# A two-layer decoder in split fp32: the first MLP's step list with chunk 0 behind the settling, twelve pairs and eight accumulating transfers

## The chip, the cores and the metric

The kernel runs on one core of one Trainium2 chip. Its engines are PE (TensorE: matrix products), DVE (VectorE), ACT (ScalarE), POOL (GpSimd) and SP (SyncE, which issues the transfers). Each engine takes its own instructions in the order in which they were written for it, and waits on semaphores for the others. SBUF is the on-chip memory, PSUM the eight banks of 128 x 512 fp32 that PE writes its sums to. The metric is device time in microseconds (us); the kernel before takes 544.23 us, the median of three runs (544.15 to 544.59).

## The reference

Two layers, each an attention and an MLP; each of the four parts ends in a residual sum and a LayerNorm. The sequence is 256 tokens of 1024 features, the hidden width of the MLP is 4096. The attentions (block-sparse in layer 0, dilated in layer 1) are not touched by the change in what they do.

```python
def sq_relu_mlp(x, w_in, w_out):
    return jnp.square(jax.nn.relu(x @ w_in)) @ w_out

    ...
    h = x
    for i in range(DEPTH):
        ...
        h = layer_norm(DEEPNORM_ALPHA * h + mix, ln_mix_g[i], ln_mix_b[i])
        h = layer_norm(DEEPNORM_ALPHA * h + sq_relu_mlp(h, mlp_w_in[i], mlp_w_out[i]),
                       ln_mlp_g[i], ln_mlp_b[i])
```

## The kernel before

**Split fp32.** PE gets every fp32 operand as two fp32r parts, a high part (`hi`, a copy in the shorter format) and a low part (`lo`, what is left), and forms three products: hi by hi, hi by lo, lo by hi. So each weight tile costs ACT one copy (`whi<-raw`) and DVE one subtraction (`wlo<-raw,whi`), both 128 x 1024, after SP has loaded it into one of six `raw` buffers. The parts lie in ten `whi` and ten `wlo` slots (`NSLOT`); a new weight waits until PE is done with the one ten earlier. `load_w(..., by_dma=True)` makes the low part in another way: ACT writes -hi into `wlo` (line 414) and a POOL transfer adds the weight to it in memory (line 416), so DVE is not needed; a tile so loaded has the letter `d` in the step list.

**The order of work.** Every operation is recorded with its buffers, and `Plan.order` schedules all of them by written-down costs and latencies: on each engine the operation that can start first comes first, and of several the one with the earliest due time. `NUDGE` shifts the due times of single operations by their number. The result is a fixed order for each engine; the tile names in it carry the number of the buffer.

**The MLP.** Its hidden width is cut into eight chunks of 512, each of four tiles of 128 columns. The step list of `STEPS`, one string for each layer's MLP, is read by `Mlp.rest`:

- Chunk 0's first product runs in `head` and `half`, token by token, half of the 256 tokens at a time.
- `w1` multiplies chunk 1's four tiles by x in four of the PSUM banks called `tp`; `f30` multiplies one tile (chunk 3, tile 0) in one of the four banks called `acc`. For each tile ACT copies half of the bank (`tz<-acc`) and DVE adds the other half (`tz<-acc,tz`), which frees the bank. After every second tile ACT takes relu, the square and the high part (`ahi`), DVE the low part (`alo`).
- `00` is the plain second product of chunk 0's first two tiles of 128 hidden features: 24 matmuls of 128 x 512 into the four sums `acc[m][n]` (token half m, output half n).
- `1A` and `1B` are the second product of chunk 1's first and second two tiles as a Strassen-like pair: seven products of 128 x 512 for eight, so 21 matmuls. They need sums of weights (`load_pair`) and of activations (`side_sums`; their parts lie in `e` buffers) from DVE, and add up in four side banks (the four `tp`) and three of the `acc` sums. The fourth, `acc[1][1]`, is not used by a pair.
- `.3` lets PE do three of the pair's seven products that wait in `todo`, which spreads them between the `f` tiles.
- `drain` adds `acc[1][1]` to the residual and gives its bank free: it is then the one bank through which all `f` tiles rotate. One `f` tile can start only when DVE has added the one before it out of that bank.
- `settle` brings the four side banks into the residual `xtok` (`tok` in the profile).
- Plain steps behind it are not multiplied at their place but collected in `tail`; `out_and_ln` does them output piece by output piece, so that the LayerNorm of the first 128 tokens can begin while PE still works on the others.

## Time and profile before

| | |
|---|---|
| median of three runs | 544.23 us (544.15 to 544.59) |
| profiled execution | 544.48 us |
| span of its trace | 542.7 us |
| granted TensorE clock | 0.997 |
| busy: PE, DVE, ACT, POOL | 534.1, 511.8, 376.8, 12.3 us |
| first MLP's second products and tiles | some 133 to 283 us of the span |
| second MLP's | some 390 to 535 us |

The page of the profile gives busy times, the chain of work that ended last, and groups of instructions by line (a helper's line stands for all that call it, so tiles say more than lines). The timeline lists the instructions of an engine in order of time; like neighbours are merged, with their count at the end. Its first number is the start in us, its second the duration. Matmuls overlap, so the time that one costs is the distance from its start to the next start, not its duration. In brackets stands how long the engine had been idle, and what released it.

### The profile page before, as it was taken

What the parts mean: (1) busy time and instruction counts of PE and PEld (TensorE: products, weight loads), DVE (VectorE), ACT (ScalarE), POOL (GpSimd) and SP (SyncE); (2) the same over time, 40 slices, a digit from 0 to 9 for tenths busy, and PEclk for the clock granted to TensorE, in tenths of its full rate; (3) what the DMA queues carried; (4) which work ended last, traced back from release to release, by engine and by line L of the source; (5) the groups of instructions that cost most, each with busy time, mean ns of one, the idle gap of its engine ahead of it and who ended that gap; (6) DMA issues with size and microseconds to landing.
All of it is one profiled execution on the core that took longest, in us unless ns stands there. A gap on an engine that the chain in (4) does not pass through costs nothing.

```text
span 542.7 us, 9038 instructions
## 1 busy us (share of the span) xinstructions
PE 534.1 (98%) x3398; PEld 452.9 (83%) x3398; DVE 511.8 (94%) x839; ACT 376.8 (69%) x616; POOL 12.3 (2%) x19
## 2 busy tenths in 40 slices
PE   9999999999999999999999999999999999999994
PEld 7888888888888888888878988888888888888883
DVE  6899999798999999999899899989999999999997
ACT  6778786477776797787653655655877879797650
POOL 0000000000000000000000000000000000000001
PEclk9999999999999999999999999999999999999998
DMA  8994245629364678853853841654936685695412
GB/s 319 397 327 171 93 165 187 242 79 338 114 202 169 224 206 270 281 149 122 309 234 105 322 143 57 201 184 152 351 117 194 198 268 167 192 294 208 148 39 77
DMA packets 31259, 108.78 MB, mean 200 GB/s; under 512 B 3440, under 2 KB 4464, under 8 KB 31216
## 3 DMA queue, kind: packets, MB, share of 16 engines
q1 hardware_dynamic: 29952, 104.87, 55.8%
q0 software_dynamic: 864, 3.15, 3.0%
q8 instruction: 26, 0.43, 0.3%
q10 hardware_dynamic: 400, 0.20, 0.1%
q14 instruction: 17, 0.14, 0.1%
HBM read 107.15 MB, written 1.05 MB: 199 GB/s over the span
## 4 chain that ended last, share of the span: by engine, by line
PE 98%; DVE 1%; issue 0%; DVEq 0%
PE acc L390 66%; PE tp L390 29%; PE tp L722 1%; PE tp L739 1%; DVE tok L639 1%; DVE bst L994 0%; DVE bst L978 0%; DVE bst L972 0%; DVEq L1518 0%; DVE tok L632 0%; DVE mv L1008 0%; DVE bst L997 0%
## 5 line engine op out<-in xcount | busy, mean ns | idle before, releaser
L381 ACT ACTIVATE whi<-raw 128x1024 fp32r<-128x1024 f32 (+2 forms) x180 | 181.8, 1035 | 51.8 <-PE acc L390 24.1
L386 DVE TENSOR_TENSOR wlo<-raw,whi 128x1024 fp32r<-128x1024 f32 (+2 forms) x180 | 210.0, 1194 | 5.3 <-ACT whi L381 3.5
L390 PE MATMUL acc<-xs,whi 128*128 128x512 f32 (+1 forms) x560 | 136.1, 387 | 0.0
L390 PEld LDWEIGHTS acc<-xs,whi 128*128 128x128 f32 x560 | 103.6, 190 | 22.2 <-ACT whi L381 0.7
L390 PE MATMUL acc<-xs,wlo 128*128 128x256 f32 x544 | 76.3, 283 | 0.0
L390 PEld LDWEIGHTS acc<-xs,wlo 128*128 128x128 f32 x544 | 73.1, 192 | 3.6
L390 PE MATMUL acc<-whi,ahi 128*128 128x512 f32 (+1 forms) x151 | 55.4, 394 | 0.0
L390 PE MATMUL acc<-wlo,ahi 128*128 128x512 f32 (+1 forms) x151 | 55.1, 388 | 0.0
L390 PE MATMUL acc<-whi,alo 128*128 128x512 f32 (+1 forms) x151 | 54.7, 388 | 0.0
L390 PE MATMUL tp<-whi,e 128*128 128x512 f32 x138 | 48.5, 390 | 0.0
L390 PEld LDWEIGHTS acc<-whi,alo 128*128 128x128 f32 x151 | 28.4, 188 | 6.3 <-DVE alo L632 0.4
L390 PEld LDWEIGHTS acc<-whi,ahi 128*128 128x128 f32 x151 | 28.1, 188 | 6.0 <-ACT ahi L1075 0.4
L390 PEld LDWEIGHTS acc<-wlo,ahi 128*128 128x128 f32 x151 | 28.4, 188 | 5.4
L381 ACT ACTIVATE whi<-m 128x1024 fp32r<-128x1024 f32 x23 | 24.3, 1056 | 12.3 <-DVE m L632 11.2
L632 DVE TENSOR_TENSOR tz<-acc,tz 128x256 f32<-128x256 f32 x68 | 27.9, 418 | 3.3 <-ACT tz L647 2.5
L390 PE MATMUL tp<-xs,whi 128*128 128x512 f32 x128 | 30.2, 391 | 0.0
L390 PEld LDWEIGHTS tp<-whi,e 128*128 128x128 f32 x138 | 26.0, 188 | 5.1
L390 PE MATMUL acc<-whi,xs 128*128 128x512 f32 (+1 forms) x112 | 28.7, 364 | 0.0
L386 DVE TENSOR_TENSOR wlo<-m,whi 128x1024 fp32r<-128x1024 f32 x23 | 28.0, 1218 | 0.1
L390 PEld LDWEIGHTS tp<-xs,whi 128*128 128x128 f32 x128 | 23.9, 188 | 4.9
L632 DVE TENSOR_TENSOR m<-raw,raw 128x1024 f32<-128x1024 f32 x23 | 27.9, 1215 | 0.0
L390 PE MATMUL tp<-wlo,e 128*128 128x512 f32 x69 | 27.0, 392 | 0.0
(127 smaller groups left out, 825.0 us busy)
## 6 DMA issues: line engine op xcount, KB each, us to landing
raw<-in_win_dram SPq DMA_DIRECT2D x64, 512.0 KB, 4.6
raw<-in_wout_dram SPq DMA_DIRECT2D x64, 512.0 KB, 5.0
raw<-in_wqk_dram SPq DMA_DIRECT2D x24, 512.0 KB, 5.6
raw<-in_wo_dram SPq DMA_DIRECT2D x14, 512.0 KB, 3.4
raw<-in_wv_dram SPq DMA_DIRECT2D x8, 512.0 KB, 8.1
wlo<-in_win_dram POOLq DMA_DIRECT2D x6, 512.0 KB, 9.4
g<-in_lng_dram SPq DMA_DIRECT2D x4, 512.0 KB, 6.5
b<-in_lnb_dram SPq DMA_DIRECT2D x4, 512.0 KB, 7.1
```

Of the source, the lines that this page charges most:

```text
L381: op("ACT", act(n, sbuf=sbuf), lambda: nc.scalar.activation(hi(), src(), AF.Copy), r, whi, keen=keen)
L386: lambda: nc.vector.tensor_tensor(lo(), src(), f32(hi()), op=ALU.subtract), list(r) + list(whi), wlo,
L390: nc.tensor.matmul(out_ap, lhsT, rhs, start=start, stop=stop)
L632: op("DVE", dve(n) + extra, lambda: nc.vector.tensor_tensor(out_ap(), a(), b(), op=alu), r, w)
L639: lambda: nc.vector.scalar_tensor_tensor(dst(), a(), s(), b(), op0=o0, op1=o1), r, w,
L722: nc.tensor.transpose(ps.t[:, c : c + P], src(), ident.t)
L739: nc.tensor.transpose(ps.t[:, 32 * i : 32 * i + 32], src()[c, :], ident.t[c, c])
```

## The change

The step list of the first MLP is replaced; that of the second stays.

- `00` and `01` go behind `settle`. Nothing is in the four sums before the pairs, so `drain` goes too, and the banks of the sums are taken only when the first product needs them (`bank(m, n)`). The plain tail becomes chunk 0 and chunk 7, eight k-tiles, where it was six (`61 70 71`); which plain steps are tail is now told by `settled`, not by `TAIL`.
- Chunk 2 is still multiplied as a whole, but as `W2`: into the four `acc` banks, not the `tp` banks, which the pairs now take as soon as chunk 1 has left them.
- All of chunks 1 to 6 are pairs: twelve, where chunk 6's second half was plain.
- Eight `f` tiles are loaded with the accumulating transfer, where two were.
- Chunk 0's activations must now last through the whole MLP. They lie in two of four `e` buffers of 2 x 512, which replace eight of 512; the pairs' activation sums and the attentions' probabilities get halves of such buffers (`Part`). This holds for both MLPs.
- The table `NUDGE` is another one altogether, for numbers from 222 to 2436 in place of 385 to 2447, so that the order shifts in both layers.

```diff
--- before.py
+++ after.py
@@ class Plan: which accesses of a buffer depend on each other
+class Part:
+
+
+    def __init__(self, buf, k):
+        self.buf, self.k = buf, k
+
+    @property
+    def t(self):
+        return self.buf.t[:, self.k, :]
+
+
+def touches(a, b):
+    if a is None or b is None or a == b:
+        return True
+    if isinstance(a, tuple) and isinstance(b, tuple) and a[0] == b[0] == "part":
+        return a[1] == b[1] and (a[2] is None or b[2] is None or a[2] == b[2])
+    return False
+
...
+                if isinstance(b, Part):
+                    b, key = b.buf, ("part", b.k, key)
-                    if key is None or k is None or k == key:
+                    if touches(k, key):
...
 STEPS = (
-    "w1 00 w2 01 drain f30 1A .3 f31 .3 f32 1B .3 f33 .4 f40 2A .3 f41 .3 f42 2B .3 f43 .4 f50 3A .3 f51 .3 f52d "
-    ".3 f53 3B .4 f60 .3 f61 4A .3 f62d .3 f63 4B .4 f70 .3 f71 5A .3 f72 .3 f73 5B .4 6A settle 61 70 71 ",
+    "w1 W2 f30 1A .4 f31d 1B .4 f32 .4 f33d 2A .5 f40 .4 f41d 2B .4 f42 3A .4 f43d .5 f50 3B .4 f51d .4 f52 4A .4 "
+    "f53d 4B .5 f60 .4 f61d 5A .4 f62 .4 f63d 5B .5 f70 6A .4 f71 .4 f72 6B .4 f73 .4 settle 00 01 70 71 ",
     "w1 00 w2 01 drain f30 1A .4 f31 1B .4 f32d .4 f33 2A .5 f40 .4 f41 2B .4 f42d 3A .4 f43 .5 f50 3B .4 f51 .4 "
     "f52d 4A .4 f53 4B .5 f60 .4 f61 5A .4 f62d .4 f63 5B .5 f70 6A .4 f71 .4 f72 6B .4 f73 .4 settle 70 71 ",
 )
...
-    385: 20.75, 418: 9.25, 468: 14.55, 593: 6.3, 604: 12.3, 891: 10.55, 907: 1.65, 974: 12.15, 1032: -14.25, 1046:
...
+    222: 5.95, 237: 6.85, 244: 5.15, 604: 2.8, 717: -5.4, 763: 25.95, 771: -17.45, 788: 19.1, 797: 9.15, 805:
...
-            hi, lo = [mk([P, 512], F32R, "e", 8) for _ in range(2)]
+            t = mk([P, 2, 512], F32R, "e", 4)
+            hi, lo = [Part(t, k) for k in range(2)]
...
-    def mm_pair(act, sums, weights, acc, side, last):
+    def mm_pair(act, sums, weights, bank, side, last):
...
             lambda: product(pure(0, 0), full[0], 0, p1),
-            lambda: product(mixed(1), full[0], 512, acc[0][1][0]),
+            lambda: product(mixed(1), full[0], 512, bank(0, 1)),
             lambda: product(mixed(2), full[1], 0, p5),
             lambda: product(mixed(0), full[1], 512, p7),
             lambda: product(mixed(3), full[2], 0, p6),
-            lambda: product(pure(1, 0), full[2], 512, acc[0][0][0]),
-            lambda: product(pure(1, 1), tail, 0, acc[1][0][0]),
+            lambda: product(pure(1, 0), full[2], 512, bank(0, 0)),
+            lambda: product(pure(1, 1), tail, 0, bank(1, 0)),
         ]
...
-            self.chunks = {c: act_tiles() for c in range(nx)}
+            self.chunks = {c: tuple(mk([P, 4, S], F32R, "e", 4) for _ in range(2)) for c in range(nx)}
...
-            acc = new_acc()
-            side = [psum("tp") for _ in range(4)] if "w" not in STEPS[i] else None
+            acc, side, settled = [[None, None] for _ in range(2)], None, False
+
+            def bank(m, n):
+                if acc[m][n] is None:
+                    acc[m][n] = (psum("acc"), n * 512, 512)
+                return acc[m][n][0]
+
             nkt = DFF // P
-            ntail = TAIL[2 * i + 1]
             tail, sums, todo, boths = [], {}, [], {}
             steps = STEPS[i].split()
             left = len(WPAIRS[i])
@@ -1155,11 +1185,11 @@
 
             plain_left = sum(x[0].isdigit() and x[1] in "01" for x in steps[: steps.index("drain")]) if "drain" in steps else 0
             for step in steps:
-                if step[0] == "w":
+                if step[0] in "wW":
                     c = int(step[1])
                     opened(c)
                     ws = [load_w(win[i][c * 4 + j]) for j in range(4)]
-                    pss = [psum("tp") for _ in range(4)]
+                    pss = [psum("tp" if step[0] == "w" else "acc") for _ in range(4)]
                     mm_wide(pss, ws)
                     for j, ps in enumerate(pss):
                         squared(c, j, ps)
@@ -1174,32 +1204,34 @@
                 elif step[0] == ".":
                     some(int(step[1:]))
                 elif step == "drain":
-                    z, bank = xtok[1], acc[1][1][0]
-                    stt(512, 0, lambda: z.t[:, 512:], lambda: z.t[:, 512:], lambda: ALPHA, lambda: bank.t, ALU.mult, ALU.add,
-                        [(z, 1), bank], [(z, 1)])
-                    drained = True
+                    z, full = xtok[1], bank(1, 1)
+                    stt(512, 0, lambda: z.t[:, 512:], lambda: z.t[:, 512:], lambda: ALPHA, lambda: full.t, ALU.mult, ALU.add,
+                        [(z, 1), full], [(z, 1)])
+                    drained, acc[1][1] = True, None
                 elif step == "settle":
                     some(len(todo))
                     settle(side, ALPHA, drained)
-                    if drained:
-                        acc[1][1] = (psum("acc"), 512, 512)
+                    bank(1, 1)
+                    settled = True
                 elif step[1] in "AB":
                     if side is None:
                         side = [psum("tp") for _ in range(4)]
                     c, n = int(step[0]), "AB".index(step[1])
                     pos = c * 4 + 2 * n
                     left -= 1
-                    todo += mm_pair((*chunks[c], 2 * n), sums[c, n], load_pair(wout[i][pos], wout[i][pos + 1]), acc, side, not left)
+                    todo += mm_pair((*chunks[c], 2 * n), sums[c, n], load_pair(wout[i][pos], wout[i][pos + 1]), bank, side, not left)
                 else:
                     c, n = int(step[0]), int(step[1])
                     for k in range(2):
                         pos = c * 4 + 2 * n + k
                         item = ((*chunks[c], 2 * n + k), load_w(wout[i][pos]), pos, nkt)
-                        if nkt - pos <= ntail:
+                        if settled:
                             tail.append(item)
                             continue
                         plain_left -= 1 if k else 0
                         for m in range(2):
+                            for side_n in range(2):
+                                bank(m, side_n)
                             mm_rows(acc[m], item, m, (acc[1][1][0],) if plain_left == 0 and k and m else ())
             out_and_ln(acc, tail, len(tail), gb, self.last, between)
```

In the whole program PE has three 128 x 512 matmuls fewer (1758 to 1755), and its other counts are equal. DVE has six subtractions `wlo<-raw,whi` fewer and the twelfth pair's own operations more; ACT has six `wlo<-raw` copies more; POOL has twelve accumulating transfers for six.

**Where the pairs begin, on PE.** In the names, the two buffers behind the arrow are the one that PE loads and the one that it streams. Before, the end of `01` (into `acc_254` and `acc_255`), the first products of pair 1A (`tp_324`, `acc_253`) and the first `f` tile (`acc_321`):

```order
L390 MATMUL acc_254_1881<-whi_314_1802,alo_239_1720 128x512
L390 MATMUL acc_255_1883<-whi_314_1802,alo_239_1720 128x512
L390 MATMUL tp_324_2080<-whi_331_1836,ahi_256_1878 128x512
L390 MATMUL tp_324_2080<-wlo_332_1894,ahi_256_1878 128x512
L390 MATMUL tp_324_2080<-whi_331_1836,alo_257_1913 128x512
L390 MATMUL acc_253_1868<-whi_331_1836,e_276_1929 128x512
L390 MATMUL acc_253_1868<-wlo_332_1894,e_276_1929 128x512
L390 MATMUL acc_253_1868<-whi_331_1836,e_277_1938 128x512
L390 MATMUL acc_321_2093<-xs0_1_76,whi_319_1818 128x512 x4
L390 MATMUL acc_321_2093<-xs1_2_77,whi_319_1818 128x512 x4
L390 MATMUL acc_321_2093<-xs0_1_76,wlo_320_1889 128x256 x4
L390 MATMUL acc_321_2093<-xs1_2_77,wlo_320_1889 128x256 x4
```

Now, the end of the wide chunk 2 (`acc_281`, `acc_282`) and the first products of 1A:

```order
L415 MATMUL acc_281_1877<-xs0_1_76,wlo_273_1723 128x256 x4
L415 MATMUL acc_281_1877<-xs1_2_77,wlo_273_1723 128x256 x4
L415 MATMUL acc_282_1887<-xs0_1_76,wlo_276_1732 128x256 x4
L415 MATMUL acc_282_1887<-xs1_2_77,wlo_276_1732 128x256 x4
L415 MATMUL tp_296_1989<-whi_303_1753,ahi_244_1894 128x512
L415 MATMUL tp_296_1989<-wlo_304_1772,ahi_244_1894 128x512
L415 MATMUL tp_296_1989<-whi_303_1753,alo_245_1926 128x512
L415 MATMUL tp_297_2002<-whi_305_1794,e_264_1928 128x512
L415 MATMUL tp_297_2002<-wlo_306_1802,e_264_1928 128x512
L415 MATMUL tp_297_2002<-whi_305_1794,e_264_1928 128x512
```

The pairs follow chunk 2's tiles directly, and chunk 2's tiles stand in `acc` banks that the pairs' sums need next.

**The rotating bank.** PE now, from the end of the second `f` tile (`acc_315`) through products of the pairs to the third (`acc_333`):

```order
L415 MATMUL acc_315_2081<-xs0_1_76,wlo_314_1860 128x256 x4
L415 MATMUL acc_315_2081<-xs1_2_77,wlo_314_1860 128x256 x4
L415 MATMUL acc_328_2114<-whi_307_1804,ahi_244_1894 128x512
L415 MATMUL acc_328_2114<-wlo_308_1857,ahi_244_1894 128x512
L415 MATMUL acc_328_2114<-whi_307_1804,alo_245_1926 128x512
L415 MATMUL acc_329_2121<-v_309_1819,ahi_244_1894 128x512
L415 MATMUL acc_329_2121<-v_310_1831,ahi_244_1894 128x512
L415 MATMUL acc_329_2121<-v_309_1819,alo_245_1926 128x512
L415 MATMUL tp_296_1989<-whi_345_1970,ahi_266_2035 128x512
L415 MATMUL tp_296_1989<-wlo_346_2020,ahi_266_2035 128x512
L415 MATMUL tp_296_1989<-whi_345_1970,alo_267_2050 128x512
L415 MATMUL acc_333_2135<-xs0_1_76,whi_331_1937 128x512 x4
```

DVE now, from its add of the first `f` tile (`acc_293`) to its add of the second, which gives the bank to `acc_333`:

```order
L657 TENSOR_TENSOR tz_295_2056<-acc_293_2022,tz_295_2056 128x256
L411 TENSOR_TENSOR wlo_348_2064<-m1_344_1995,whi_347_2048 128x1024
L411 TENSOR_TENSOR wlo_350_2074<-raw_343_1882,whi_349_2061 128x1024
L411 TENSOR_TENSOR wlo_357_2086<-raw_355_1973,whi_356_2069 128x1024
L657 TENSOR_TENSOR raw_342_1871<-raw_343_1882 128x512
L657 TENSOR_TENSOR m1_368_2106<-raw_366_1999,raw_367_2027 128x1024
L411 TENSOR_TENSOR wlo_370_2119<-raw_366_1999,whi_369_2110 128x1024
L657 TENSOR_TENSOR tz_295_2056<-acc_315_2081,tz_295_2056 128x256
```

DVE before, up to its add of the first `f` tile (`acc_321`), with the drain (`acc_255`) in it:

```order
L639 SCALAR_TENSOR_TENSOR tok_118_345<-tok_118_345,acc_255_1883 128x512
L632 TENSOR_TENSOR raw_349_1852<-raw_350_1902 128x512
L386 TENSOR_TENSOR wlo_373_2098<-raw_371_1981,whi_372_2085 128x1024
L632 TENSOR_TENSOR tz_305_2009<-tz_305_2009 128x4x128
L632 TENSOR_TENSOR tz_305_2009<-tz_305_2009 128x2x128
L386 TENSOR_TENSOR v_359_2122<-raw_349_1852,v_358_2100 128x512
L632 TENSOR_TENSOR alo_287_2128<-tz_305_2009,ahi_286_2045 128x1024
L632 TENSOR_TENSOR tz_323_2130<-acc_321_2093,tz_323_2130 128x256
```

Between the two adds DVE now has five operations of 1024 columns and one of 512; PE has the second tile and some products of two pairs.

**The end of the program, on DVE.** Before, from the last but one write of the residual to the last add of a sum (`tp_1137`):

```order
L639 SCALAR_TENSOR_TENSOR tok_118_345<-tok_118_345,t1_1119_5902 128x512
L632 TENSOR_TENSOR tok_118_345<-tok_118_345,t1_1119_5902 128x512
L639 SCALAR_TENSOR_TENSOR tok_117_339<-pt_1136_5977,rstd_1134_5991,b_1073_5497 128x512
L639 SCALAR_TENSOR_TENSOR tok_118_345<-tok_118_345,acc_788_4629 128x512
L639 SCALAR_TENSOR_TENSOR tok_117_339<-pt_1136_5977,rstd_1134_5991,b_1073_5497 128x512
L994 BN_STATS bst_1140_6022<-tok_118_345 128x6
L639 SCALAR_TENSOR_TENSOR tok_118_345<-tok_118_345,acc_1120_6003 128x256
L978 BN_STATS bst_1140_6022<-tok_118_345 128x6
L994 BN_STATS bst_1140_6022<-tok_118_345 128x6
L632 TENSOR_TENSOR tok_118_345<-tok_118_345,tp_1137_5980 128x256
```

Now, to the same add (`tp_1107`):

```order
L664 SCALAR_TENSOR_TENSOR pt_1106_5965<-tok_113_339,mv_1103_5963,g_1042_5467 128x512 x2
L1031 TENSOR_SCALAR rstd_1104_5975<-sums_1105_5954 128x1
L664 SCALAR_TENSOR_TENSOR tok_114_345<-tok_114_345,acc_795_4630 128x512
L1020 BN_STATS bst_1110_5989<-tok_114_345 128x6
L664 SCALAR_TENSOR_TENSOR tok_113_339<-pt_1106_5965,rstd_1104_5975,b_1043_5472 128x512 x2
L664 SCALAR_TENSOR_TENSOR tok_114_345<-tok_114_345,acc_1090_5977 128x256
L1004 BN_STATS bst_1110_5989<-tok_114_345 128x6
L1020 BN_STATS bst_1110_5989<-tok_114_345 128x6
L657 TENSOR_TENSOR tok_114_345<-tok_114_345,tp_1107_5991 128x256
```

The settling's last two operations (the first two rows before) now stand further ahead, and both writes `tok_113<-pt` stand behind the add of `acc_795`, where one of the two stood ahead of it. On PE, 24 matmuls of 128 x 256 follow that sum now; 21 did before.

17 lines of the change are left out of this document (9 added, 8 removed), and 16 rows, old and new, of the table NUDGE.

## The prediction

> **What bounds the kernel now.** I read the page first: the busy shares and the chain that ended last.
>
> ```profile
> span 542.7 us, 9038 instructions
> PE 534.1 (98%) x3398; PEld 452.9 (83%) x3398; DVE 511.8 (94%) x839; ACT 376.8 (69%) x616; POOL 12.3 (2%) x19
> PE 98%; DVE 1%; issue 0%; DVEq 0%
> ```
>
> PE bounds the run, DVE stands four points behind it. An average says little for a change in one stage, so next the windows, with their columns PE, PEld, DVE, ACT, POOL, clock, DMA share, GB/s: the way into the first MLP's pairs, the first MLP up to the settling, and the second MLP.
>
> ```profile
> 118.00:163.00 45.00, 45.00 (x239) 38.72 (x238) 41.98 (x51) 33.13 (x50) 0.00 (x0) 1.00 0.64 211
> 133.00:283.00 150.00, 149.97 (x764) 127.30 (x763) 146.40 (x192) 113.19 (x163) 2.46 (x3) 1.00 0.64 213
> 390.00:525.00 135.00, 135.00 (x685) 115.10 (x684) 133.35 (x170) 104.28 (x152) 3.48 (x4) 1.00 0.61 192
> ```
>
> PE has no hole in either MLP and runs at full clock. So time is won there only by giving PE fewer or cheaper instructions, and lost when DVE, 97% busy in the second row, hands something over late. The second MLP already runs the step list that the first gets in its middle (twelve pairs), and no wait of PE shows there.
>
> Two handovers show how much room there is. Each `f` tile writes one rotating `acc` bank; the next `f` tile must wait until DVE has added the last one out. The timeline of PE and DVE at the second `f` tile of the first MLP (164.01 is its first matmul, 163.16 the add that frees its bank), and at a like place in the second MLP:
>
> ```profile
> 159.18 1.98 PE L390 MATMUL acc<-xs,whi 128*128 128x512 f32 x8
> 161.00 1.12 PE L390 MATMUL acc<-xs,wlo 128*128 128x256 f32 x8
> 161.95 0.40 PE L390 MATMUL tp<-whi,e 128*128 128x512 f32 x1
> 164.01 1.98 PE L390 MATMUL acc<-xs,whi 128*128 128x512 f32 x8
> ...
> 158.02 0.69 DVE L639 SCALAR_TENSOR_TENSOR tok<-tok,acc 128x512 f32<-128x512 f32 x1
> 158.63 0.69 DVE L632 TENSOR_TENSOR raw<-raw 128x512 f32<-128x512 f32 x1
> ...
> 163.16 0.42 DVE L632 TENSOR_TENSOR tz<-acc,tz 128x256 f32<-128x256 f32 x1
> 163.50 1.21 DVE L386 TENSOR_TENSOR wlo<-raw,whi 128x1024 fp32r<-128x1024 f32 x1
> ...
> 417.42 0.41 DVE L632 TENSOR_TENSOR tz<-acc,tz 128x256 f32<-128x256 f32 x1
> 417.75 0.68 DVE L632 TENSOR_TENSOR raw<-m,raw 128x512 f32<-128x512 f32 x1
> ...
> 418.13 2.02 PE L390 MATMUL acc<-xs,whi 128*128 128x512 f32 x8
> ```
>
> DVE's add is over at 163.50 and at 417.75 (the next start), PE needs the bank at 164.01 and 418.13: 0.5 and 0.4 us to spare. The first rows also give pitches: eight 512-wide matmuls in 161.00 - 159.18, 0.227 us each, eight 256-wide in 0.95, 0.12 each. For DVE, from start to start, 256 columns cost 0.34 (163.16 to 163.50) and 512 cost 0.61 (158.02 to 158.63); 1024 cost 1.14, as a group of three is 1.13 longer than one of two (3.48 and 2.35, quoted below).
>
> **The matmuls.** The twelfth pair does with 21 matmuls what plain step 61 did with 24, 512 wide all of them; the other counts are equal. Nothing covers PE here, so 3 x 0.227 = **-0.68 us**.
>
> **Chunk 0's 48 matmuls.** They leave the place ahead of the pairs and come behind the settling: 48 x 0.227 = 10.9 us of PE work that moves, nothing won or lost by itself. But they were cheap for DVE: four weight splits, 4 x 1.14 = 4.6 us. Without them DVE must have the pairs' operands 6.3 us earlier against its own work. DVE's accumulated lateness decides. First its anchor and its idle time before:
>
> ```profile
> 118.53 0.40 PE L390 MATMUL tp<-wlo,xs 128*128 128x512 f32 x1
> 120.13 0.60 PE L722 MATMUL tp<-ident,t 128*128 128x128 f32 x4
> 120.48 0.48 PE L390 MATMUL tp<-whi,xs 128*128 128x512 f32 x1
> ...
> 119.76 2.35 DVE L386 TENSOR_TENSOR wlo<-raw,whi 128x1024 fp32r<-128x1024 f32 x2
> 127.93 3.48 DVE L386 TENSOR_TENSOR wlo<-raw,whi 128x1024 fp32r<-128x1024 f32 x3
> 133.18 1.22 DVE L386 TENSOR_TENSOR wlo<-raw,whi 128x1024 fp32r<-128x1024 f32 x1 [1.76 <-PE tp L390]
> ```
>
> PE at 118.53 is in chunk 0's second half (its second matmul); DVE at 119.76 is done with the LayerNorm. Both points lie ahead of what moves. In the new order the tightest place is the third `f` tile (`acc_333` in the order rows above), whose bank DVE frees with its add from `acc_315`. On PE there lie, from 118.53 on, 139 matmuls of 512 columns, 80 of 256 and eight transposes (0.09 each: 120.13 to 120.48 for four): 31.55 + 9.6 + 0.7, and 0.1 at either turn to transposes and back. So PE wants the bank at about 160.6. On DVE there lie 24 operations of 1024 columns, 14 of 512 and 12 of 256: 27.4 + 8.5 + 4.1 = 40.0, so the add ends at 159.7 if DVE never idles, 0.9 us ahead. In the old order the same sum to the add at 163.16 is 25, 13 and 11: 40.1, or 159.9, while it came at 163.16: DVE lost 3.3 us, 1.76 of them in the one wait at 133.18 for a slot that PE held.
>
> So the wait at the third `f` tile lies between nothing (DVE loses under 0.7 us) and 2.6 us (it loses 3.3 us again). I went through DVE's rows with ACT's beside them: the wait of 1.76 goes, since the order now puts the adds of chunk 1 and the next sums where that slot is awaited, but DVE still waits a few tenths for ACT three or four times, for the copies of v, the squares and the high parts of chunk 1, 1.1 us in all by my count. Then the add ends at 160.8 and PE waits, with 0.2 us from one to the other, some **+0.4 us**. That value lies nearer the low end, as the second MLP's 0.4 us to spare does.
>
> **Eight accumulating transfers for two.** Each takes one split off DVE (1.14) and puts one copy on ACT (1.05). Rows for both sides, the POOL issue, and the transfer:
>
> ```profile
> L414 ACT ACTIVATE wlo<-raw 128x1024 fp32r<-128x1024 f32 x6 | 6.3, 1049 | 0.1
> q0 software_dynamic: 864, 3.15, 3.0%
> wlo<-in_win_dram POOLq DMA_DIRECT2D x6, 512.0 KB, 9.4
> DMA to landing us min/median/max: 7.8/9.4/10.3
> 195.00:210.00 15.00, 15.00 (x78) 12.80 (x78) 14.80 (x19) 13.18 (x20) 0.00 (x0) 1.00 0.92 282
> ```
>
> ACT goes from 113.2 to about 119.5 of these 150 us by the six copies, still with a fifth of its time free; DVE loses 6 x 1.14 = 6.8 us and gets 4.3 back, most of it the twelfth pair's own sums and splits, by the order's rows at their pitches. Neither is on PE's path beyond what the last part counted: **0**. A transfer that lands late would be: by the sums above the first is issued about 137.5 and its tile is needed at 157.6, 20 us for a landing of at most 10.3. Six more transfers at 3.0% / 6 of 542.7 us each take 16 us of the engines' 96 (0.64 x 150), share 0.75; single stretches stand at 0.92 already.
>
> On this side the Trainium skill, SBUF — State Buffer, section "SBUF: two separate sides", speaks against the change: a DMA issued from GpSimd can be starved of its descriptors while DVE holds the port that the two share, and it advises the hardware queues. The six landings here, beside a DVE that is 97% busy, bear out no such starving of more than a few us, and only a landing of twice the longest would cost PE time.
>
> **The first MLP's LayerNorm.** The plain tail grows from six k-tiles to eight. The old place, where PE reached the transposes before DVE had their input:
>
> ```profile
> 277.07 0.69 DVE L985 SCALAR_TENSOR_TENSOR tok<-tok,acc 128x512 f32<-128x512 f32 x1
> ...
> 281.15 0.39 PE L390 MATMUL acc<-wlo,ahi 128*128 128x512 f32 x1
> 281.57 0.66 PE L722 MATMUL tp<-ident,tok 128*128 128x128 f32 x4
> ...
> 282.98 0.40 PE L390 MATMUL acc<-wlo,ahi 128*128 128x512 f32 x1
> ```
>
> From DVE's last add to the transposes it takes 281.57 - 277.07 = 4.5 us; with the matmul's own 0.39 that is 4.9. PE stood 0.19 us (281.57 - 281.15 - 0.227). In the new order 24 matmuls, 5.4 us, lie between the end of token half 0's sum and its transposes: the 0.19 can go, but the two last weights wait for slots that the tail itself holds, and one split of 1.14 us too late costs 1.14 - 0.5 = 0.6. Bounds -0.2 and +0.6, taken as **0**: no row is nearer to one bound than to the other.
>
> **The end.** The steps of the second MLP stay, but the new table orders the end otherwise, and behind it nothing hides:
>
> ```profile
> 527.54 0.39 PE L390 MATMUL acc<-whi,alo 128*128 128x512 f32 x1
> 532.00 0.39 PE L390 MATMUL acc<-whi,alo 128*128 128x512 f32 x1
> 532.23 0.28 PE L390 MATMUL acc<-whi,ahi 128*128 128x256 f32 x1
> 534.62 0.28 PE L390 MATMUL tp<-whi,alo 128*128 128x256 f32 x1
> ...
> 532.43 0.69 DVE L639 SCALAR_TENSOR_TENSOR tok<-tok,acc 128x512 f32<-128x512 f32 x1
> 533.03 0.74 DVE L639 SCALAR_TENSOR_TENSOR tok<-pt,rstd,b 128x512 f32<-128x512 f32 x1
> 535.14 0.40 DVE L632 TENSOR_TENSOR tok<-tok,tp 128x256 f32<-128x256 f32 x1
> ```
>
> Now the add at 532.43 starts with the end of its sum (532.39) and 2.71 us later, at 535.14, comes the last add, 0.24 behind PE's end (534.90). In the new order the sum ends 24 matmuls of 256 before the end, 2.88 us, and between the two adds stands one more write of a normalized half (0.67, the row at 533.03 to the next). So the last add comes 2.71 + 0.67 - 2.84 = 0.54 behind PE's end: **+0.30 us**, bounds 0 (DVE catches up) and 0.7.
>
> **Sum.** -0.68 + 0.4 + 0 + 0 + 0.30 = 0.02, on the profiled execution's 544.48 (span 542.7 and 1.78 around it). The median of the runs, 544.23, lies 0.25 lower; with the same offset the changed kernel's median is **544.2**.
>
> **Rivals.**
>
> *No wait at the first pairs.* DVE loses under 0.7 us on the way; for it speaks that six splits leave DVE. Then -0.68 + 0.30: 543.85. Against it: any loss of more than that, and it lost 3.3.
>
> *DVE becomes the bound at the first pairs* (the slower side). It loses 3.3 us again between 119.76 and the third `f` tile, PE stands there for 2.6: -0.68 + 0.30 + 2.6 = +2.2, 546.4. It decides the result from about 1.5 us of standing (544.23 - 0.38 + 1.5 = 545.35). For it: 41.98 busy of 45 in the window; against it: the wait of 1.76 has another place, and twelve pairs in the second MLP run without a hole.
>
> *The LayerNorm gains as well.* No wait at the pairs, the last add at 0.24 as before, and the standing around the transposes gone: 0.19 ahead of them, and 0.24 in the 1.41 us to 282.98, in which stand eight transposes (0.72) and two matmuls (0.45). Then -0.68 - 0.43: 543.1. Against it: the table has moved the end, and the longer tail moves more on DVE.
>
> *The accumulating transfers land late.* At a DMA share of 0.92 a landing could take twice its 10.3 us; then a tile waits about a microsecond, two or three times over: 545.5 to 547. The slack of 20 us speaks against it. The port rule of the Trainium skill's page named above would work at the same place and give the same time.
>
> *The change does not do what it says*: PE's count in the order is three matmuls lower, so this is out but for the -0.68 being hidden behind a wait, which is the second rival.
>
> **How the numbers follow.** 0.2% of 544.23 is 1.09 us, about what a measurement of this kernel tells from no change: 543.14 and 545.32 are the bounds. Forecast 0.46, no wait 0.25, DVE the bound 0.15, LayerNorm gains 0.11, late transfers 0.03. The first two are "same", 0.71; the gain at 543.1 stands on the bound and is given to "faster" with most of its weight and a little of the second case, 0.12; slower has 0.17 with part of DVE's case below its full price. The range: all savings and no cost give 543.2, the forecast with a wait of 1.8 instead of 0.4 gives 545.6; beyond these lie about 2 in 10.
>
> **What would show it.** Right: PE's idle before the third `f` tile a few tenths, 45 of 45 busy elsewhere in both MLPs; PE's last matmul about 0.3 us earlier (-0.68 + 0.4), and the last add 0.5 behind it. Wrong: a standing PE of more than 1.5 us between 140 and 170 us, a PE wait on a POOL transfer, or a last matmul over 1 us earlier or later.

## The result and the profile after

The changed kernel takes **548.01 us**, the median of six runs (546.37 to 548.48); the kernel before takes 544.41 us (six runs, 543.92 to 545.55). The ratio is 1.0056 with a 95% interval of 1.0038 to 1.0074: slower by 3.0 to 3.6 us, where 544.2 and "no change" had been forecast.

The page of the changed kernel: span, busy times, transfer queues (packets, MB, share of 16 engines' time), and the chain that ended last by engine. Line numbers are 25 higher than before in this part of the code: L415 is the matmul, L411 DVE's split, L406 ACT's copy, L439 and L441 are ACT's negative copy and POOL's transfer; in the experiments' kernels the same lines stand some places off.

```profile
span 546.3 us, 9045 instructions
...
PE 534.7 (98%) x3395; PEld 452.7 (83%) x3395; DVE 511.1 (94%) x837; ACT 383.5 (70%) x625; POOL 19.1 (3%) x25
...
q1 hardware_dynamic: 29952, 104.87, 55.9%
q0 software_dynamic: 1728, 6.29, 6.1%
...
PE 81%; DVE 9%; DMA 4%; ACT 3%; issue 2%; POOL 0%; DVEq 0%; ACTq 0%
```

PE has three matmuls fewer, as worked out. But the chain was 98% PE before and is 81% now; DVE, DMA and ACT have come into it. PE's waits in the changed kernel (total us, times, longest) say where:

```profile
PE acc L415 <- DMA wlo<-in_win_dram: 1.5, 1, 1.5
...
PE acc L415 <- DVE tz L657: 0.6, 2, 0.3
PE acc L415 <- DVE xs L411: 0.3, 1, 0.3
```

The first MLP of the changed kernel by the windows (columns as in the prediction: window, its length, PE, PEld, DVE, ACT, POOL, clock, DMA share, GB/s):

```profile
133.00:283.00 150.00, 149.67 (x767) 127.75 (x767) 144.21 (x189) 118.87 (x174) 8.61 (x9) 1.00 0.73 227
```

ACT and the DMA share are close to what was worked out (119.5 us and 0.75).

The busy times hide what a matmul loses while the last one still drains, so I made a ledger of PE's losses: for every two matmuls, the distance from start to start less the median distance of its kind in the kernel before, added up by stretch. The ledger is of the profiled execution; the last column is the median of the runs, from which that execution lies up to 1.6 us away (e3: 549.29 profiled, 550.92 the median). The borders are times of each trace, so in kernels that are late there, work of the first MLP falls into the column behind it: 2.3 us of e11's 11.9.

| kernel | to 118 | first MLP, 118-292 | attention, 292-388 | from 388 | us |
|---|---|---|---|---|---|
| before | 18.2 | 1.7 | 9.0 | 0.4 | 544.4 |
| changed | 18.2 | 2.2 | 10.6 | 2.1 | 548.0 |
| e1, one ACT copy earlier | 18.6 | 2.5 | 9.1 | 0.6 | 546.0 |
| e2, old table from the first MLP's end | 18.1 | 1.2 | 9.3 | 4.3 | 549.6 |
| e3, before with the new table from there | 17.9 | 0.8 | 9.0 | 4.4 | 550.9 |
| e4, new buffers alone | 22.4 | 3.1 | 9.4 | 4.3 | 556.4 |
| e5, e1 with eight small transfers | 18.2 | 1.3 | 9.0 | 0.5 | 544.6 |
| e9, e1 with one small transfer | 18.8 | 1.2 | 9.2 | 0.5 | 544.7 |
| e10, e1 with that transfer later | 18.2 | 2.4 | 9.0 | 0.8 | 546.3 |
| e6, before, no table | 18.5 | 3.3 | 9.7 | 11.4 | 558.4 |
| e7, changed, no table | 19.2 | 14.3 | 10.5 | 11.5 | 569.6 |
| e8, e7 with two transfers | 18.9 | 17.4 | 10.7 | 11.7 | 573.1 |
| e11, e7 with chunk 0 first | 18.3 | 11.1 | 11.9 | 11.5 | 568.0 |

Tenths of the first column are the start of the program: in the profiles of e1, e9, e10 and some others PE waits 0.3 to 1.2 us for the high part of a weight at 8 us, in those of before, changed and e5 it doesn't.

From before to the changed kernel the ledger gives +3.8 us; with -0.68 for three matmuls and +0.43 at the end (below) it is +3.6, as the two profiled executions differ (548.11 - 544.48). The places:

**The second MLP, 1.7 us.** Its step list is the old one, yet its last accumulating transfer comes late. The timeline of PE, POOL and ACT in the changed kernel, and then the landing of that transfer from the tile's view (us, minimum, median, maximum of one):

```profile
492.67 1.98 PE L415 MATMUL acc<-xs,whi 128*128 128x512 f32 x8
496.12 1.22 PE L415 MATMUL acc<-xs,wlo 128*128 128x256 f32 x8 [1.47 <-DMA wlo<-in_win_dram]
...
486.33 0.86 POOL L441 DMA_DIRECT2D wlo<-in_win_dram  x1 [30.98 <-ACT wlo L439]
...
481.36 1.04 ACT L438 ACTIVATE whi<-raw 128x1024 fp32r<-128x1024 f32 x1
...
484.99 1.05 ACT L439 ACTIVATE wlo<-raw 128x1024 fp32r<-128x1024 f32 x1
```

```profile
DMA to landing us min/median/max: 9.7/9.7/9.7
```

The same transfer in the kernel before, with its first use and ACT's two copies, and its landing:

```profile
481.18 0.86 POOL L416 DMA_DIRECT2D wlo<-in_win_dram  x1 [24.97 <-ACT wlo L414]
...
477.16 1.04 ACT L413 ACTIVATE whi<-raw 128x1024 fp32r<-128x1024 f32 x1
...
479.84 1.05 ACT L414 ACTIVATE wlo<-raw 128x1024 fp32r<-128x1024 f32 x1
...
493.78 1.11 PE L390 MATMUL acc<-xs,wlo 128*128 128x256 f32 x8
```

```profile
DMA to landing us min/median/max: 10.3/10.3/10.3
```

Before, it landed at 481.18 + 10.3 = 491.5, 2.3 us ahead of its use. Now it lands at 486.33 + 9.7 = 496.0, where PE, after eight matmuls of 0.227, would have used it at 494.5. It is issued 5.1 us later because ACT's copies for this tile come later: the high part at 481.36 in place of 477.16, the negative copy 3.63 us behind that in place of 2.68, with four other copies between. The new table has an entry (2290: 39.65) that puts off just this negative copy, but without that entry the planner's order moves it up by one ACT instruction only: most of the 5.1 us comes from the order as a whole (and 0.7 from PE, which is later by that much when it comes to this tile). From issue to first use this transfer had 12.6 us before, the least of the six accumulating transfers (the others 16.4 to 20.5, by the order beside the trace); now it has 8.2 to the time at which PE would have used it.

**The first MLP, 0.5 us at 190.** There is no wait at the third `f` tile, where the prediction had one. DVE's add and PE's next matmul into the bank, in the changed kernel:

```profile
160.50 0.42 DVE L657 TENSOR_TENSOR tz<-acc,tz 128x256 f32<-128x256 f32 x1
...
161.09 2.00 PE L415 MATMUL acc<-xs,whi 128*128 128x512 f32 x8
```

The wait comes 30 us later. In the order SP, POOL, ACT, DVE, PE, from the timeline of the changed kernel:

```profile
176.76 1.16 SPq L402 DMA_DIRECT2D raw<-in_win_dram  x2
...
179.33 2.59 SPq L402 DMA_DIRECT2D raw<-in_wout_dram  x2
...
177.03 0.88 POOL L441 DMA_DIRECT2D wlo<-in_win_dram  x1 [18.08 <-ACT wlo L439]
...
186.44 1.06 ACT L406 ACTIVATE whi<-raw 128x1024 fp32r<-128x1024 f32 x1 [0.81 <-DMA raw<-in_win_dram]
...
187.53 1.23 DVE L411 TENSOR_TENSOR wlo<-raw,whi 128x1024 fp32r<-128x1024 f32 x1 [0.42 <-ACT whi L406]
...
190.73 0.42 DVE L657 TENSOR_TENSOR tz<-acc,tz 128x256 f32<-128x256 f32 x1 [0.24 <-ACT tz L1091]
...
191.21 2.12 PE L415 MATMUL acc<-xs,whi 128*128 128x512 f32 x8 [0.33 <-DVE tz L657]
```

Five transfers of 512 KB start within 5 us, one of them an accumulating one. The second plain load takes 8.8 us to land (loads at a like place before: 3.8 to 5.3), ACT's copy waits for it, DVE's split for ACT, the add that frees the rotating bank stands behind the split on DVE, and PE waits for the bank. The transfers' view of the changed kernel for 176 to 183 us (last number: median us to landing):

```profile
raw<-in_win_dram SPq DMA_DIRECT2D x2, 512.0 KB, 6.2
raw<-in_wout_dram SPq DMA_DIRECT2D x2, 512.0 KB, 7.6
wlo<-in_win_dram POOLq DMA_DIRECT2D x1, 512.0 KB, 9.1
```

**The attention of layer 1, 1.6 us.** This is not steady: e1, e2, e5, e9 and e10 stand at 9.0 to 9.3 there, as before did, the changed kernel's profile alone of these at 10.6, although PE's order up to 355 us is the same in all of them. The changed kernel's six runs lie in two groups, 546.4 and 546.6 against 548.0 to 548.5, which would fit a loss that comes and goes; only one run has a profile, so this isn't shown, and the cause stays open.

**The end, 0.43 us.** DVE's last adds in the changed kernel, whose last matmul ends at 538.05:

```profile
536.28 1.40 DVE L664 SCALAR_TENSOR_TENSOR tok<-pt,rstd,b 128x512 f32<-128x512 f32 x2
...
538.72 0.41 DVE L657 TENSOR_TENSOR tok<-tok,tp 128x256 f32<-128x256 f32 x1
```

The last add comes 0.67 behind PE's end, 0.24 before: two writes of normalized halves in place of one stand between.

### The profile page after: what moved, and what is told of

It reads as the page before. It is cut to its first block, busy times and chain, and to the rows that moved or that the text cites. A ratio compares the mean times of both kernels' runs of the same rounds, so it can differ in the third digit from the quotient of the medians.

```text
span 546.3 us, 9045 instructions
## 1 busy us (share of the span) xinstructions
PE 534.7 (98%) x3395; PEld 452.7 (83%) x3395; DVE 511.1 (94%) x837; ACT 383.5 (70%) x625; POOL 19.1 (3%) x25
## 3 DMA queue, kind: packets, MB, share of 16 engines
q1 hardware_dynamic: 29952, 104.87, 55.9%
q0 software_dynamic: 1728, 6.29, 6.1%
HBM read 110.30 MB, written 1.05 MB: 204 GB/s over the span
## 4 chain that ended last, share of the span: by engine, by line
PE 81%; DVE 9%; DMA 4%; ACT 3%; issue 2%; POOL 0%; DVEq 0%; ACTq 0%
PE acc L415 54%; PE tp L415 25%; DVE wlo L411 2%; DMA wlo<-in_win_dram 2%; ACT whi L406 2%; DMA raw<-in_win_dram 2%; DVE tz L657 2%; DVE tok L664 1%; PE tp L747 1%; DMA raw<-in_wqk_dram 1%; DVE e L723 1%; PE tp L764 1%; DVE tz L411 0%; DVE t L657 0%; ACT tz L1099 0%
## 5 line engine op out<-in xcount | busy, mean ns | idle before, releaser
L406 ACT ACTIVATE whi<-raw 128x1024 fp32r<-128x1024 f32 (+2 forms) x174 | 176.2, 1034 | 49.9 <-PE acc L415 19.4
L411 DVE TENSOR_TENSOR wlo<-raw,whi 128x1024 fp32r<-128x1024 f32 (+2 forms) x174 | 203.1, 1194 | 4.6 <-ACT whi L406 3.8
L415 PE MATMUL acc<-xs,whi 128*128 128x512 f32 (+1 forms) x592 | 144.8, 389 | 0.9 <-DVE tz L657 0.6
L415 PEld LDWEIGHTS acc<-xs,whi 128*128 128x128 f32 x592 | 109.3, 190 | 25.6 <-DVE tz L657 2.1
L415 PE MATMUL acc<-xs,wlo 128*128 128x256 f32 x576 | 80.8, 284 | 1.5 <-DMA wlo<-in_win_dram 1.5
L415 PEld LDWEIGHTS acc<-xs,wlo 128*128 128x128 f32 x576 | 77.2, 192 | 5.6 <-DMA wlo<-in_win_dram 1.9
L415 PE MATMUL tp<-whi,e 128*128 128x512 f32 x144 | 50.9, 391 | 0.0
L415 PE MATMUL acc<-whi,ahi 128*128 128x512 f32 (+1 forms) x112 | 43.1, 393 | 0.0
L415 PE MATMUL acc<-wlo,ahi 128*128 128x512 f32 (+1 forms) x112 | 43.0, 389 | 0.0
L415 PE MATMUL acc<-whi,alo 128*128 128x512 f32 (+1 forms) x112 | 42.7, 387 | 0.0
L415 PE MATMUL acc<-whi,e 128*128 128x512 f32 x112 | 38.6, 391 | 0.0
L406 ACT ACTIVATE whi<-m 128x1024 fp32r<-128x1024 f32 x24 | 25.3, 1056 | 12.5 <-DVE m L657 9.8
L415 PEld LDWEIGHTS tp<-whi,e 128*128 128x128 f32 x144 | 27.1, 188 | 5.5
L411 DVE TENSOR_TENSOR wlo<-m,whi 128x1024 fp32r<-128x1024 f32 x24 | 29.3, 1219 | 0.5 <-ACT whi L406 0.4
L415 PE MATMUL acc<-whi,xs 128*128 128x512 f32 (+1 forms) x112 | 28.8, 365 | 0.0
L415 PE MATMUL tp<-wlo,e 128*128 128x512 f32 x72 | 28.2, 392 | 0.0
L1091 ACT ACTIVATE tz<-acc 128x256 f32<-128x256 f32 x44 | 16.2, 371 | 15.5 <-PE acc L415 15.5
L415 PE MATMUL tp<-whi,xs 128*128 128x512 f32 x80 | 25.6, 400 | 0.0
L415 PEld LDWEIGHTS acc<-whi,ahi 128*128 128x128 f32 x112 | 21.1, 188 | 4.3 <-issue 0.3
L415 PEld LDWEIGHTS acc<-whi,alo 128*128 128x128 f32 x112 | 21.1, 188 | 4.3
```

The lines of the kernel that those rows point to most:

```text
L406: op("ACT", act(n, sbuf=sbuf), lambda: nc.scalar.activation(hi(), src(), AF.Copy), r, whi, keen=keen)
L411: lambda: nc.vector.tensor_tensor(lo(), src(), f32(hi()), op=ALU.subtract), list(r) + list(whi), wlo,
L415: nc.tensor.matmul(out_ap, lhsT, rhs, start=start, stop=stop)
L1091: op("ACT", act(S), lambda: nc.scalar.activation(one(), ps.t[:, S:], AF.Copy), [ps], [key])
```

## The experiments

**One ACT instruction earlier.** The negative copy of the late tile moves up on ACT, past the four copies between, right behind its high-part copy; nothing else changes.

```diff
+MOVES = ((2289, 2290, 2291),)
...
-        return [o for _, _, o in done]
+        return self.early([o for _, _, o in done])
+
+    def early(self, ops):
+        for first, *rest in MOVES:
+            moved = [o for o in ops if o.n in rest]
+            ops = [o for o in ops if o.n not in rest]
+            at = [o.n for o in ops].index(first) + 1
+            ops[at:at] = moved
+        return ops
```

> The changed kernel with one ACT instruction moved: the negative copy of the tile that the last accumulating transfer of the second MLP completes stands right behind the copy of its high part, five instructions earlier, so that the transfer is issued some 2.7 us earlier; nothing else moves on any engine. Theory A (the changed kernel loses most where this transfer lands after PE has come to the tile: PE stood 1.6 us at 494): 1.3 to 1.7 us less than the changed kernel, about 546.4, no PE wait on the transfer, and runs closer together than the 546.4 to 548.5 of the changed kernel. Theory B (the transfers are slow because DMA or DVE is busy, and the wait only moves): the transfer lands late again by a microsecond or more, 547.5 to 548.2.

Measured: 545.96 us (ten runs, 543.86 to 547.08), ratio to before 1.0019 (1.0005 to 1.0033). The timeline of e1, the transfer and its use:

```profile
482.88 0.86 POOL L452 DMA_DIRECT2D wlo<-in_win_dram  x1 [28.30 <-ACT wlo L450]
...
493.93 1.12 PE L426 MATMUL acc<-xs,wlo 128*128 128x256 f32 x8
```

It is issued 3.5 us earlier, and PE no longer waits for it. So the late transfer is the larger part of the loss: 2.0 us by the medians (0.8 to 3.3 by the intervals of the two ratios), 1.5 in the ledger; the other 0.5 is not placed. The runs scatter no less than those of the changed kernel, against the expectation. What is left is the wait at 190, larger in this execution, and one at the start of the program, at 8 us (PE's waits in e1):

```profile
PE acc L426 <- DVE tz L668: 0.8, 1, 0.8
PE acc L426 <- ACT whi L417: 0.8, 1, 0.8
```

**Whose part is it, the table's or the step list's?** The part of the table behind the first MLP (from operation 1346, old numbers 28 lower) is exchanged: e2 is the changed kernel with the old part, e3 the kernel before with the new part.

```diff
 NUDGE: (e2)
-    the changed kernel's entries from 1346 on
+    the entries of before from 1318 on, each number + 28
 NUDGE: (e3, in the kernel before)
-    its entries from 1318 on
+    the changed kernel's entries from 1346 on, each number - 28
```

> The changed kernel with the old table's entries for all operations behind the first MLP (renumbered by 28), its own for the rest. Theory A (the new table's second part costs the late transfer, 1.6 us, and the later last add, 0.4): 2.0 us less than the changed kernel, about 546. Theory C (the whole loss behind the first MLP, 3.7 us, comes from that part of the table): 544.0 to 544.4. Theory D (the larger e buffers and chunk 0's activations in them cost it, whatever the table): 547 to 548.

> The kernel before with the new table's entries for all operations behind the first MLP (renumbered by 28): no change to the first MLP and to the buffers. Theory A: 2.0 us more than before, about 546.4, with a PE wait on the last accumulating transfer. Theory C: 547.5 to 548. Theory D: as before, 544.2 to 544.6.

Measured: e2 549.57 us, ratio 1.0089 (1.0068 to 1.0111); e3 550.92 us, 1.0118 (1.0087 to 1.0148). PE's waits, of e2 and then of e3:

```profile
PE tp L414 <- DVE alo L656: 1.6, 1, 1.6
PE acc L414 <- DVE tz L656: 1.2, 2, 0.9
```

```profile
PE acc L391 <- DMA wlo<-in_win_dram: 2.3, 1, 2.3
```

e3 shows that the new table makes the transfer late in the old kernel too: it is the table's doing, and no step of the list is needed for it. Theory A had this sign, but not the size: e3 loses 6.3 us by the medians. Of the 4.8 in its profiled execution 2.3 are the wait and 2.0 stand behind PE's last matmul, which the ledger doesn't count: the last add starts 2.27 us behind it (539.97 against 537.70), where it was 0.24 before.

No theory had e2 at 549.6; in the profiled executions it is as slow as the changed kernel (548.11 both). The old part doesn't fit any more: it makes DVE late, and PE waits for it at 486 and 489 us, though the second MLP's steps and operations are the same. It isn't the new list that it fails to fit. e4, the next experiment, has the old list and the old table in the changed code, and it has the same two waits; from 340 us of e2 on, PE's order in the two is the same for all 1064 matmuls left, and it is another than before's. So the changed `e` buffers and banks are enough to turn the old entries into another order.

**The buffers alone.** The changed code with the old step list and the old table, so that only the four double `e` buffers and the later taking of banks are new.

```diff
 STEPS[0], NUDGE:
-    those of the changed kernel
+    those of the kernel before
```

> The changed kernel's buffers alone: e buffers as four of two halves with chunk 0's activations in two of them, the banks of the sums taken lazily, but the step list and the table of the kernel before. Theory D (the buffers hold layer 1 and the second MLP back): 1.5 to 2 us more than before, 546 to 546.5, with PE waits between 288 and 385 us. Theories A and C: within 0.3 us of before.

Measured: 556.4 us, 1.0222 (1.0202 to 1.0242), far more than was expected. 4.3 us of it is one new wait at the head of the first MLP, and the second MLP has e2's waits:

```profile
PE tp L743 <- issue: 4.6, 2, 4.3
PE tp L411 <- DVE alo L653: 1.6, 1, 1.6
PE acc L411 <- DVE tz L653: 1.2, 2, 0.9
```

No theory had this: there is no PE wait between 288 and 385 us, where theory D had it. That doesn't price the buffers, since the old table meets an order it wasn't made for. So both tables went:

```diff
 NUDGE = {
-    ...
 }
 (e6: the kernel before; e7: the changed kernel;
  e8: e7 with the letter d in the first list on f52 and f62 alone)
```

> The kernel before with the table of shifts empty: the planner's own order. A base for the next two. Slower than before by some us (546 to 552), by waits of PE that the table took away.

> The changed kernel with the table empty: step list and buffers alone. Theory H (the step list is itself worth -0.5 to -1.5 us in the first MLP, and the buffers cost nothing): 0.5 to 1.5 us less than e6_before_no_table. Theory D (the buffers cost time in layer 1 and the second MLP): 1 to 4 us more than e6_before_no_table, the loss behind 288 us.

> As e7_after_no_table, but in the first MLP only the tiles f52 and f62 are loaded with the accumulating transfer, as in the kernel before; the other six splits are DVE's again. Theory I (DVE, with 6.8 us more work and no cushion ahead of the pairs, becomes the bound in the first MLP; this is what the transfers are for): 2 to 6 us more than e7_after_no_table, with PE waiting on DVE between 140 and 280 us. Theory F (the transfers cost more than they give): 0 to 1 us less.

Measured: e6 558.39 us, 1.0249 (1.0233 to 1.0264); e7 569.6 us, 1.0459 (1.0441 to 1.0477); e8 573.08 us, 1.052 (1.0506 to 1.0535). The windows of 133 to 283 us, of e6, e7 and e8:

```profile
133.00:283.00 150.00, 149.31 (x759) 126.53 (x757) 144.43 (x190) 111.76 (x161) 3.37 (x3) 1.00 0.61 205
```

```profile
133.00:283.00 150.00, 142.36 (x709) 118.01 (x708) 137.15 (x176) 114.19 (x166) 7.14 (x8) 0.99 0.71 222
```

```profile
133.00:283.00 150.00, 139.89 (x694) 114.67 (x693) 142.18 (x180) 107.94 (x158) 1.90 (x2) 0.99 0.59 200
```

Theories H and D both fail: e7 is 11 us slower than e6, and the loss lies in the first MLP. Three readings. In the second MLP e6 and e7 lose the same (11.4 and 11.5 in the ledger), and PE's last 632 matmuls, from 413 us of e6 on, stand in the same order: under an empty table the new buffers change and cost nothing there. In the first, in the planner's own order, the new list loses 11 us more than the old (14.3 against 3.3), mostly in waits for DVE; the new table's entries take nearly all of that back. And the six more accumulating transfers are worth 3.1 us in that order (17.4 against 14.3), as theory I had it, for they take splits off a DVE that is late: they aren't a mere cost.

**Is it chunk 0's move that makes DVE late?** e7 with chunk 0 ahead of the pairs again (and chunk 2 in the `tp` banks, as before).

```diff
-    "w1 W2 f30 1A .4 f31d 1B ... settle 00 01 70 71 ",
+    "w1 00 w2 01 drain f30 1A .4 f31d 1B ... settle 70 71 ",
```

> As e7_after_no_table (empty table, new buffers, twelve pairs, eight accumulating transfers), but chunk 0's second product stands ahead of the pairs again (w1 00 w2 01 drain ... settle 70 71). Theory K (the 10.9 us of PE work that need little of DVE, moved away from the front, are what makes DVE late: the first MLP lost 14.1 us in e7 and 2.7 in e6): the first MLP loses 2 to 5 us, the whole 9 to 12 us less than e7_after_no_table, 558 to 561. Theory L (the twelve pairs or the transfers do it): within 3 us of e7_after_no_table, 567 to 570.

Measured: 568.02 us, 1.0433 (1.0405 to 1.046), 1.6 us under e7. That is theory L's time; where the loss lies agrees with it in part only. PE's longest sums of waits between 118 and 310 us, in e7 and in e11:

```profile
PE acc L405 <- DVE tz L647: 5.6, 7, 2.0
PE tp L405 <- DVE alo L647: 2.0, 2, 1.5
```

```profile
PE acc L405 <- DVE tz L647: 4.2, 5, 2.0
PE tp L405 <- DVE alo L647: 2.1, 2, 1.5
PE tp L737 <- DVE tok L654: 1.9, 1, 1.9
```

The waits between the pairs begin later (at 227 in place of 199 us) and are fewer, and a new one comes at the LayerNorm's transposes, ahead of which the tail is short again. Counted between the same numbers of matmuls instead of the same times, PE loses 13.8 us in e7 and 9.1 in e11 from the 990th, near 118 us, to the 1785th, shortly ahead of these transposes (2.5 in e6, to the 1788th), and 0.9 and 4.3 from there to the end of the first MLP. So the move has some 4.7 of the 11.3 us by which the pairs of e7 are worse than e6's, and what comes with it, the longer tail, gives 3.5 back. The rest lies in what the two lists share: the twelve pairs, their spacing and the transfers' place in the order. Which of the three stays open.

**The transfers' bytes.** e1, in which the eight accumulating transfers of the first MLP move 64 of 1024 columns; every instruction stays in its place. e9 does so for the one at 177 us alone (operation 967).

```diff
+            n = 64 if len(plan.ops) < 1400 else 1024        (e5)
+            n = 64 if len(plan.ops) == 967 else 1024        (e9)
-            op("POOL", SWDGE, lambda: nc.gpsimd.dma_start(lo(), src.bitcast(F32R), accum_op=ALU.add), ...
+            op("POOL", SWDGE, lambda: nc.gpsimd.dma_start(lo()[:, :n], src[:, :n].bitcast(F32R), accum_op=ALU.add), ...
```

> The kernel of e1_copy_early with every instruction where it stands, but the first MLP's eight accumulating transfers carry 64 of 1024 columns each, so the low parts of these eight weight tiles are left unfinished (their other columns hold the negative high part) and the output is not the reference's; what is measured is the kernel with 1/16 of these transfers' bytes. Theory F (their bytes hold up the plain loads beside them: the load that ACT waits for at 186 lands 8.8 us after its issue, with the DMA engines full, and passes its lateness on to DVE and to the rotating bank at 190 to 192, where PE stood 0.5 to 1.0 us): the wait at 190 goes, 0.5 to 1.0 us less than e1_copy_early, about 545.1, and runs closer together. Theory G (the wait at 190 comes from the order on ACT and DVE alone): as e1_copy_early, 545.7 to 546.2.

> As e5_small_transfers, but only one of the eight transfers of the first MLP is cut to 64 columns: the one issued at 177, together with the loads for which ACT waits at 186 (the low part of that one weight tile stays unfinished, so the output is not the reference's). Theory F1 (this one collision costs the 1.2 us between e1_copy_early and e5_small_transfers): about 544.7 to 545.0, a ratio to before of about 1.000, no PE wait at 190. Theory F2 (all eight cost a little each, by loads that come late in places that differ from run to run): 545.4 to 546, less than a third of the way.

Measured: e5 544.61 us (eleven runs), ratio to before 0.9997 (0.9989 to 1.0006); e9 544.69 us (eleven runs), 1.0001 (0.9992 to 1.0009); by the ratios 1.2 and 1.0 us under e1. The transfers of e9 at 176 to 183 us:

```profile
raw<-in_win_dram SPq DMA_DIRECT2D x2, 512.0 KB, 4.1
raw<-in_wout_dram SPq DMA_DIRECT2D x2, 512.0 KB, 4.4
wlo<-in_win_dram POOLq DMA_DIRECT2D x1, 32.0 KB, 5.2
```

With 32 KB in place of 512 in one transfer the four loads beside it land in 4.1 and 4.4 us (6.2 and 7.6 in the changed kernel, medians of two), and PE doesn't wait at 190. One collision carries as much as all eight, within an interval of some 0.9 us on either difference; the other seven transfers' bytes cost nothing that can be seen. It isn't the same in every execution: e2 has the same five transfers there, loads of 5.5 and 6.2 us at the median, and no wait at 190. Its later pair of loads:

```profile
raw<-in_wout_dram SPq DMA_DIRECT2D x2, 512.0 KB, 6.2
```

**Issuing that transfer later.** e1, with the negative copy of the tile at 177 moved three ACT instructions down.

```diff
-MOVES = ((2289, 2290, 2291),)
+MOVES = ((2289, 2290, 2291), (999, 966, 967))
```

> The kernel of e1_copy_early with one more ACT instruction moved, and full transfers: the negative copy of the tile of the transfer at 177 stands three instructions later, so that the transfer is issued some 2.3 us behind the two loads with which it collided; its tile is needed at 193. Theory F1: the loads land first, the wait at 190 goes or shrinks to 0.2, 0.5 to 1.0 us less than e1_copy_early, ratio to before about 1.000 to 1.001. Theory J (the engines stay full until 187 whatever comes first, and the transfer now comes late for its own tile): as e1_copy_early or up to 1 us slower, with a PE wait on the transfer at 193.

Measured: 546.28 us, 1.0031 (1.0019 to 1.0043), no better than e1 (545.96). The transfer starts 3.0 us later than in e1 (180.54 against 177.57). The wait for the bank stays, only the load that is late is another: the one issued at 181.6 takes 8.4 us and lands at 190.0, and DVE's sum of two weights starts right behind it (the view names DVE as the releaser, whose own work had ended 0.98 us before). DVE in e10's timeline, and then the windows with the DMA share (0.96, 1.01, 1.04):

```profile
190.09 1.23 DVE L668 TENSOR_TENSOR m<-raw,raw 128x1024 f32<-128x1024 f32 x1 [0.98 <-DVE raw L668]
```

```profile
181.00:184.00 3.00, 3.00 (x19) 2.64 (x18) 2.87 (x5) 1.84 (x5) 0.41 (x1) 1.00 0.96 225
184.00:187.00 3.00, 3.00 (x15) 2.48 (x14) 3.00 (x4) 3.00 (x4) 0.00 (x0) 1.00 1.01 254
187.00:190.00 3.00, 3.00 (x19) 2.64 (x18) 2.11 (x3) 2.98 (x6) 0.87 (x1) 1.00 1.04 274
```

With the 16 engines full for 9 us (the next loads start at 187.6), another order of the issues changed only which transfer was late. That is theory J, but for the wait at 193, which isn't there.

No version here beats the kernel before: with the late copy mended it is 1.0019, and even with that one transfer's bytes gone 1.0001. These two together are what the forecast missed in sum, for 1.0001 (0.9992 to 1.0009) is where it had the changed kernel.

## Why the prediction was wrong

- **Matmuls, -0.68: right.** Three fewer, and PE's pitch is the same.
- **The second MLP: no term, the step that failed.** The sum has a term for that MLP's end and nothing for the rest of it, since its step list stays and no wait of PE showed there. But the table by itself is a change of that stage (e3). The transfer with the least room in the kernel before, 2.3 us between landing and use (491.5 against 493.78), stood there; the new order has ACT's copy for it later, and PE stands for 1.5 us. That cost 2.0 us by e1's medians, 1.5 by the ledger. The order is fixed when the program is made, so it could have been read without a run.
- **"Eight accumulating transfers for two: 0": the other step that failed.** It worked out the slack of the first transfer alone ("20 us for a landing of at most 10.3"). For their own tiles this holds for all eight of the first MLP, which have 14.1 to 24.1 us from issue to first use and land in at most 10.1. But the step asked only when the accumulating transfer lands, not what it does to plain loads beside it, although the row with a DMA share of 0.92 was quoted. That cost 1.0 to 1.2 us by e5 and e9, through one of eight transfers. The Trainium skill, DMA: Bandwidth & Descriptors, section "Rules for kernel authors", says that transfers issued by different engines share the same 16 DMA engines and interleave; e9's loads (4.1 us beside a small transfer, 6.2 beside a full one) agree, and that rule, not the port rule that the prediction weighed, was the one that bore on this change. Of descriptors starved by DVE nothing shows: twelve landings took 8.4 to 10.1 us, six had taken 7.8 to 10.3.
- **The wait at the third `f` tile, +0.4: not there, and that by little.** DVE's add ends at 160.84 (160.50 and its pitch of 0.34), as worked out (160.8). But PE comes for the bank at 161.09 and not at 160.6: it begins chunk 0's second half 0.26 us later (118.79 for 118.53) and loses as much again on the way. So DVE was as late as forecast, and it is luck that PE was late too. The same chain (DVE late, rotating bank held) stopped PE at 190 for 0.5 us, but there a load made it late, not the lost 48 matmuls. In the planner's own order the move does cost time between the pairs (e11), but from 199 us on, not at the first pairs.
- **LayerNorm 0 (bounds -0.2 to +0.6): the gain was larger.** In the stretch of 260 to 288 us the ledger goes from 0.85 to 0.03. The 0.19 and the slow pitch around the transposes were seen, but 0.5 us between 270 and 272 were not looked for.
- **The end, +0.30: +0.43 measured**, by the mechanism named, bounds held.
- **Rivals.** "The accumulating transfers land late", with a chance of 0.03, came nearest: its sign in the profile, "a PE wait on a POOL transfer", was the first wait in the list, and its 545.5 to 547 was short by 1 us. Its mechanism did not come. The late transfer took 9.7 us, less than the 10.3 of before; it was issued too late, and in the other MLP. "DVE becomes the bound at the first pairs" has some truth in the planner's own order (e7, 11 us), which the table hides, though there too the waits begin only at 199 us.

With the terms as they are in the profiled executions: -0.68 matmuls, +1.7 second MLP, +1.3 first MLP without its LayerNorm (the wait at 190, 0.3 at 290.5 for x's parts, tenths at its head), -0.8 LayerNorm, +1.6 attention (unsteady), +0.4 end: +3.5 against 3.6.

## What to carry to other kernels

Where a table of due times is replaced, every stage under it has changed: compare the order of each engine in the stages whose steps are the same, and work out the slack of every transfer, last ones first (issue plus the longest landing, against first use). A transfer that takes work off an engine can be paid by the loads that share the DMA engines with it, here at one place of eight; look at each place where it starts beside others, and at who waits for these. And entries that were made for one program don't carry over whole to another, even where the steps under them are the same: the old ones lose 4.3 us of the ledger in the second MLP of e2, 0.4 in their own kernel (an empty table 11.5).
